# A hybrid SSD and S5 decoder step on one core: modulation blocks moved into the scan, the last group norms moved between output projection groups

## The chip, the core and the metric

The kernel runs on one core of a Trainium2 chip. A core has five engines that work side by side, each through its own queue in order: TensorE (PE, matmuls; its weight loads are shown apart as PEld), VectorE (DVE), ScalarE (ACT), GpSimd (POOL) and SyncE (SP, which here issues all DMAs). The metric is the device time of one execution in microseconds (us); lower is better.

## The reference, cut to what matters

One layer of a decoder for 1024 prompt tokens (one sequence) and 8 x 4 sample tokens, D = 1024, together 1056 columns. Everything is float32.

```python
mod = (silu(c) @ w_ada + b_ada)              # 6 x 1024 per sequence: sh1, sc1, g1, sh2, sc2, g2
u = rmsnorm(x, norm1_g) * (1 + sc1) + sh1
proj = u @ w_in                              # z, xBC, dt and the S5 input
y_ssd = ssd_mixer(...)                       # conv, scan over 8 chunks of 128 tokens, * silu(z)
y_ssd = y_ssd * rsqrt(mean(y_ssd^2) + eps) * norm_g     # group norm: 2 groups of 256 channels
y_s5 = s5_mixer(...)                         # complex diagonal scan, gelu, then the glu below
y_s5 = g * sigmoid(g @ w_glu + b_glu)
x = x + g1 * (concat(y_ssd, y_s5) @ w_out)   # output projection, 1024 x 1024
v = rmsnorm(x, norm2_g) * (1 + sc2) + sh2
x = x + g2 * ((silu(v @ w_gate) * (v @ w_up)) @ w_down)  # FFN, width 2816
y = rmsnorm(x, normf_g) * (1 + scf) + shf    # modulated by a second, smaller projection of c
```

## The kernel before

Every large product of float32 matrices is done as three matmuls: both factors are split into a high and a low part (high by an ACT copy, low by a subtraction on POOL or DVE), and high x high, high x low and low x high are summed in PSUM. The 1056 columns are worked in four blocks b of NB = 264 columns.

The stages and where they lie in the profiled execution: input norm and projection (up to about 240 us), S5 (to about 325 us), the last part of the SSD scan with its group norms and the glu of the S5 half (to 472.8 us), output projection (472.8 to 589.6 us), first FFN tile by a fast matrix product (7 products instead of 8; Strassen type, `ORD`), and then ten more FFN tiles `gu(j, mat)`, the down projection and the last norm.

What the change touches:

- The modulation. `mod` has 64 columns of 128 rows here (48 of the layer, 16 of the last norm). A block is loaded by `ada_load` (512 KB; name `arw` in the scan, one buffer; `ar` in the output projection, two buffers), multiplied by `ada_mm` (8 matmuls, then an ACT copy to `adasb`) and finished by `ada_fin` (one small matmul with a selection matrix, and one DVE instruction that adds c1 and multiplies by gs). In the scan `ada_a` does the first half of the block loaded last and issues the next load, `ada_b` does the second half. In the output projection `ada_dc` does the same in the middle of a group, at its matmul 12.
- The scan. `ssd_r`, `ssd_a` and `ssd_b` are the three parts of chunk c; `ssd_b(7)` is the last. `gn_sq(b)` squares and sums the gated scan output (`gac`), `gn_stat(b)` sums over channels with 6 matmuls and takes 1/sqrt on DVE by Newton steps (`rq_m`, `rq_i`, `rq_t`, result `grs`), `gn_out(b, g)` spreads `grs` over the partitions with matmuls and scales (`gf`, then the split `m` for the output projection). `glus` does n glu units (12 matmuls, a tanh on ACT named `sg`, DVE and POOL).
- The output projection. `out_group(w, m, b)` is 24 matmuls for 128 output rows and 264 columns, then `residual` (`x<-mm,mod,x` on DVE, which needs the tile `x` reloaded by `x<-xT`) and a square for the next norm. `w_out` comes in four pieces i of 1 MB.
- The first FFN tile and its successor. `dn_sums(j)` loads a piece of `w_down` and forms sums of its quarters on DVE (`ts`), which are written to memory. `gu_forms` loads 1 MB of gate or up weights (`raw<-w_gu`, `raw` has two buffers), forms sums on DVE (`arw` again) and splits them into slots that are taken in the order of the list `WS` (names `wl`, `wh`, `wf`, `wg`).

From the scan on, PE's order is that of the code (`tc.manual_schedule` for PE alone); the orders of DVE, ACT, POOL and SP are set by a scheduler, which works from a simulated time line. Pools are opened and closed in code order, and a tile whose place is reused waits for the last use of the old one.

## Time and profile before

Three runs: median 1320.55 us, 1320.35 to 1320.65. The profiled execution took 1317.78 us: a span of 1316.0 us and 1.78 us around it.

| | busy us | share of the span |
|---|---|---|
| PE | 1232.2 | 94% |
| PEld | 1165.4 | 89% |
| DVE | 891.2 | 68% |
| POOL | 630.8 | 48% |
| ACT | 505.3 | 38% |

The mean granted TensorE clock is 0.971 of full speed. PE is the engine to watch: it is idle for 83.8 us, and it is slowed where the clock is below 1.00. Idle time of another engine means nothing by itself; what matters is which of them PE waited for in a stretch. In the timeline a bracket gives the idle time before the instruction and what ended it.

### The profile page before, as it was taken

What the parts mean: (1) busy time and instruction counts of PE and PEld (TensorE: products, weight loads), DVE (VectorE), ACT (ScalarE), POOL (GpSimd) and SP (SyncE); (2) the same over time, 40 slices, a digit from 0 to 9 for tenths busy, and PEclk for the clock granted to TensorE, in tenths of its full rate; (3) what the DMA queues carried; (4) which work ended last, traced back from release to release, by engine and by line L of the source; (5) the groups of instructions that cost most, each with busy time, mean ns of one, the idle gap of its engine ahead of it and who ended that gap; (6) DMA issues with size and microseconds to landing.
All of it is one profiled execution on the core that took longest, in us unless ns stands there. A gap on an engine that the chain in (4) does not pass through costs nothing.

```text
span 1316.0 us, 26191 instructions
## 1 busy us (share of the span) xinstructions
PE 1232.2 (94%) x10165; PEld 1165.4 (89%) x10165; DVE 891.2 (68%) x1757; ACT 505.3 (38%) x1000; POOL 630.8 (48%) x626
## 2 busy tenths in 40 slices
...
GB/s 339 177 99 158 108 97 130 147 160 241 116 161 81 107 137 214 202 108 6 158 165 178 154 132 193 154 178 154 135 127 186 124 234 200 200 184 188 212 104 133
DMA packets 203741, 206.57 MB, mean 157 GB/s; under 512 B 12128, under 2 KB 177504, under 8 KB 199264
## 3 DMA queue, kind: packets, MB, share of 16 engines
...
## 4 chain that ended last, share of the span: by engine, by line
PE 64%; DVE 19%; DMA 6%; POOL 5%; issue 3%; ACT 2%; SPq 1%; ACTq 0%; DVEq 0%; POOLq 0%
PE mm L1508 45%; PE mm L120 13%; PE ps L120 3%; POOL tr L105 2%; DVE tp L105 2%; POOL W L105 1%; DVE xo L114 1%; PE nb L120 1%; DVE m L105 1%; DVE R L105 1%; DVE gf L105 1%; DVE E L105 1%; POOL wl L105 1%; PE pa L120 1%; DMA ts<-hd 1%
## 5 line engine op out<-in xcount | busy, mean ns | idle before, releaser
L1508 PE MATMUL mm<-m,wh 128*128 128x264 f32 x1376 | 190.1, 285 | 1.6 <-DVE ue L105 1.6
L1508 PEld LDWEIGHTS mm<-m,wh 128*128 128x128 f32 x1376 | 176.6, 188 | 2.2 <-DVE ue L105 1.8
L1508 PE MATMUL mm<-m,wg 128*128 128x264 f32 x802 | 113.7, 289 | 7.9 <-ACT wg L117 7.9
L1508 PEld LDWEIGHTS mm<-m,wg 128*128 128x128 f32 x802 | 105.5, 192 | 8.4 <-ACT wg L117 8.3
L105 POOL TENSOR_TENSOR wl<-raw,wh 128x1024 fp32r<-128x1024 f32 x24 | 59.8, 2491 | 91.3 <-ACT wh L117 51.8
L1508 PE MATMUL mm<-m,wf 128*128 128x264 f32 x670 | 90.8, 284 | 0.0
L1508 PEld LDWEIGHTS mm<-m,wf 128*128 128x128 f32 x670 | 85.2, 188 | 0.2 <-DVE g L105 0.2
L105 POOL TENSOR_TENSOR wl<-arw,wl 128x512 fp32r<-128x512 f32 x40 | 56.1, 1403 | 57.3 <-ACT wl L117 57.3
L1508 PE MATMUL mm<-v,wl 128*128 128x264 f32 x586 | 83.4, 285 | 0.0
L120 PE MATMUL mm<-uh,wh 128*128 128x384 f32 (+1 forms) x360 | 77.5, 341 | 4.9 <-ACT uh L117 4.4
L1508 PE MATMUL mm<-w,wl 128*128 128x264 f32 x570 | 81.3, 284 | 0.0
L120 PE MATMUL mm<-m,wh 128*128 128x264 f32 x512 | 77.2, 299 | 1.6 <-ACT sg L117 1.3
L1508 PEld LDWEIGHTS mm<-v,wl 128*128 128x128 f32 x586 | 76.5, 188 | 0.0
L120 PE MATMUL mm<-uh,wl 128*128 128x384 f32 (+1 forms) x360 | 74.5, 332 | 0.0
L1508 PEld LDWEIGHTS mm<-w,wl 128*128 128x128 f32 x570 | 74.3, 188 | 0.0
L120 PEld LDWEIGHTS mm<-m,wh 128*128 128x128 f32 x512 | 69.4, 199 | 4.6 <-issue 2.8
L120 PE MATMUL mm<-ul,wh 128*128 128x384 f32 (+1 forms) x360 | 71.8, 327 | 1.3 <-POOL ul L105 1.2
L117 ACT ACTIVATE wh<-raw 128x1024 fp32r<-128x1024 f32 (+2 forms) x60 | 50.2, 837 | 58.2 <-PE mm L1508 26.8
L120 PEld LDWEIGHTS mm<-uh,wh 128*128 128x128 f32 x360 | 60.8, 193 | 13.2 <-issue 6.9
L105 POOL TENSOR_TENSOR wg<-raw,wg 128x512 fp32r<-128x512 f32 (+2 forms) x32 | 49.6, 1549 | 37.1 <-ACT wg L117 23.5
L105 DVE TENSOR_TENSOR m<-ts,m 128x528 fp32r<-128x528 f32 (+1 forms) x50 | 42.0, 858 | 33.0 <-ACT m L117 32.6
L120 PEld LDWEIGHTS mm<-ul,wh 128*128 128x128 f32 x360 | 59.4, 189 | 4.0 <-POOL ul L105 2.8
...
## 6 DMA issues: line engine op xcount, KB each, us to landing
...
ts<-hd SPq DMA_DIRECT2D x70, 264.0 KB, 3.7
arw<-w_ada SPq DMA_DIRECT2D x27, 512.0 KB, 4.3
...
ar<-w_ada SPq DMA_DIRECT2D x21, 512.0 KB, 4.5
...
```

What stands on the lines that cost most here:

```text
L105: e.tensor_tensor(o, a, b, op)
L114: V.scalar_tensor_tensor(o, a, s, b, o0, o1)
L117: S.activation(o, a, f, bias=bias, scale=scale)
L120: T.matmul(o, l, r, start=start, stop=stop)
L1508: T.matmul(o, wv[k][1 if s == 2 else 0], xv[k][1 if s == 1 else 0], start=first and s == 0 and k == 0, stop=(s == 2 and k == n - 1), skip_ ...
```

## The change

- Modulation: seven more `ada_a`/`ada_b` pairs stand in the scan, two more `ada_a` (on another PSUM bank) between the first output groups; 35 blocks go through `arw` instead of 27, 13 through `ar` instead of 21. `ada_dc` stands in fewer output groups. The last step of a single block is an ACT instruction (scale gs, bias cg = c1 * gs) instead of a DVE one.
- The end of the scan: early scan tiles get a pool of their own, `sde`, closed after `ssd_a(7)`; in its place the first piece of `w_out` is loaded and split during the scan (low part on DVE: `v<-raw,v`). `gn_stat(2)` and all after it go into the output projection's block, with four output groups (i = 0, b = 0 and 1) between them, and `gn_out` inside these groups. Statistics are taken in pieces of 88 columns, so that no piece needs padding.
- FFN start: `dn_sums(0)` comes after `gu(1, 0)`, and `WS` begins with the slots `wl`, `wh`, `wl`, `wf` where it began with `wg`, `wg`.
- At the end `ahead(n, mp)` is called in the loop instead of ahead of it. The orders of SP and DVE there are the same as before.

The diff, cut (the left out parts give tiles of the early scan to `sde`, and take the square sums in blocks of NB columns):

```diff
--- before.py
+++ after.py
...
@@ -186,7 +187,8 @@
         d = mod[:, m0:m0 + n, :]
         sh = [128, n, 9]
         if n == 1:
-            ts(d, o, c1[:, m0:m0 + 1], P["gs"][:, m0:m0 + 1], add, mult)
+            o, d = o[:, 0], d[:, 0]
+            act(d, o, AF.Identity, bias=cg[:, m0:m0 + 1], scale=P["gs"][:, m0:m0 + 1])
...
-    def ada_a():
+    def ada_a(own=True):
 
         m = ada_next[0]
         if ada_raw[0] is not None:
-            ada_open[0] = (m, 1) + ada_mm(ada_raw[0], 1)
+            ada_open[0] = (m, 1) + ada_mm(ada_raw[0], 1, "pa" if own else psm())
             m = ada_next[0] = m + 1
         ada_raw[0] = ada_load(m, 1, st, "arw", 1)[0] if m < 64 else None
 
...
+    sde = pool("sde", side="right")
...
         if c == 8:
-            return tl(sd, shape, tag + "8")
+            return tl(sde, shape, tag + "8")
...
@@ -1102,7 +1106,10 @@
             else:
                 tt(V, hn.rearrange("p (h q) -> p h q", q=64), hprev.rearrange("p (h q) -> p h q", q=64),
                    eAt[:, 8 * c:8 * c + 8].unsqueeze(2).to_broadcast([128, 8, 64]), mult)
-                tt(V, hn, hn, pst, add)
+                if c == 7:
+
+                    hn = tl(gl, [128, 8, 136], "gq").rearrange("p i n -> p (i n)")[:, 0:512]
+                tt(V, hn, hprev, pst, add)
...
-        sg = tl(gl, [128, 384], "sg", bufs=2)[:, 0:w]
+        sg = tl(gl, [128, NB], "sg", bufs=2)
         act(sg, o[:, 0:w], AF.Tanh, bias=bg2[:, m:m + 1], scale=0.5)
         act(sg, sg, AF.Copy, 0.5, 0.5)
-        gf = tl(gl, [128, 384], "gf", bufs=2)[:, 0:w]
+        gf = tl(gl, [128, NB], "gf", bufs=3)
...
     def gn_stat(b):
...
-        rs = tl(gl, [128, 6], "grs", bufs=2)
-        rsqrt(rs, p1[:, 384:396].rearrange("p (c z) -> p c z", z=2)[:, :, 0], 6, 1.0 / 256)
+                mm(p1[0:88, 384 + i:385 + i], GN[b][g][:, 88 * c:88 * c + 88], ones[:, 0:1])
+        rs = tl(gl, [128, 6], "grs", bufs=2)[0:88, :]
+        for _ in rsqrt_steps(rs, p1[0:88, 384:396].rearrange("p (c z) -> p c z", z=2)[:, :, 0], 6, 1.0 / 256, rows=88):
+            pass
         GN[b] = rs
 
-    def gn_out(b, g):
-        c0, w = NB * b, NB
+    def gn_out(b, g, pt="nb"):
         rs = GN[b]
-        pb = nbt()
+        pb = nbt(pt)
         for c in range(3):
-            n = min(128, w - 128 * c)
-            mm(pb[:, 128 * c:128 * c + n], rs[:, 3 * g + c:3 * g + c + 1].to_broadcast([128, 128]), ident[:, 0:n])
+            mm(pb[:, 88 * c:88 * c + 88], rs[:, 3 * g + c:3 * g + c + 1].to_broadcast([88, 128]), ident[0:88, 0:88])
         for i in range(2):
             m = 2 * g + i
-            gf = tl(gl, [128, 384], "gf", bufs=2)[:, 0:w]
-            stt(gf, yT[:, m, c0:c0 + w], P["norm_g"][:, m:m + 1], pb[:, 0:w], mult, mult)
+            gf = tl(gl, [128, NB], "gf", bufs=3)
+            stt(gf, yT[:, m, NB * b:NB * b + NB], P["norm_g"][:, m:m + 1], pb[:, 0:NB], mult, mult)
             act(mx(0, m, b), gf, AF.Copy)
             tt(G, mx(1, m, b), gf, mx(0, m, b).bitcast(F32), sub)
 
...
+    def x2_load(i):
+        for hh in range(2):
+            for n in range(2):
+                dma(x2[n][:, 2 * i + hh, :], A["xT"][2 * i + hh][:, 528 * n:528 * n + 528])
+
+    def out_weights(i):
+
+        raw = raw_tile()
+        dma(raw, A["w_out"][i])
+        if i:
+            x2_load(i)
+        return [split_h(raw, h, V if i < 2 else G, None if i in (1, 2) else [tl(vb0, [128, 4 * NB], f"v{2 * h + q}", F32R)[:, 0:1024]
+                                                            for q in range(2)]) for h in range(2)]
 
...
         glu_in(0)
         ssd_yd(8)
         h = ssd_b(1, h)
+        ada_a()
         ssd_a(2)
+        ada_b()
         ssd_r(3, PV)
         glu_in(1)
         ada_a()
+        ssd_a(3)
         ada_b()
-        ssd_a(3)
         ssd_r(4, PV)
         smp_turn(0)
         glu_in(2)
         ada_a()
         h = ssd_b(2, h)
+        ada_b()
         gn_sq(0)
         smp_state(0, (0, 1))
+        ada_a()
         smp_state(0, (2, 3))
         smp_load(1)
         glu_in(3)
         ada_b()
         ssd_a(4)
+        ada_a()
         ssd_r(5, PV)
         gn_stat(0)
         h = ssd_b(3, h)
+        ada_b()
         ssd_r(6, PV)
         ada_a()
         ssd_a(5)
@@ -1316,12 +1347,16 @@
         glus(wg, 1)
         ada_b()
         smp_out(1)
+        ada_a()
         h = ssd_b(4, h)
         smp_turn(1)
+        ada_b()
         glus(wg, 1)
         ada_a()
         ssd_a(6)
+        ada_b()
         smp_state(1, (2, 3))
+        ada_a()
         ssd_r(7, PV)
         smp_state(1, (0, 1))
         ada_b()
@@ -1335,6 +1370,9 @@
         glus(wg, 2)
         ada_a()
         ssd_a(7)
+        close("sde")
+        vb0 = pool("vb0")
+        wo0 = out_weights(0)
         gn_stat(1)
         ada_b()
         h = ssd_b(6, h)
@@ -1344,31 +1382,14 @@
         ada_b()
         h = ssd_b(7, h)
         gn_sq(3)
-        gn_stat(2)
-        gn_out(1, 1)
-        gn_out(1, 0)
-        glus(wg, 2)
-        gn_stat(3)
-        gn_out(2, 0)
-        gn_out(2, 1)
-        glus(wg, 2)
-        gn_out(3, 0)
-        gn_out(3, 1)
+        ada_a()
     dma(O["ssdp"], h)
-    ada_next[0] += 1
-    ada_fin(ada_next[0] - 1, 1, *ada_mm(ada_raw[0], 1))
-    ada_more(40 - ada_next[0])
     close("sd")
...
+        ws = {0: wo0}
+        x2_load(0)
+        gn_stat(2)
+        ada_b()
+        out_group(ws[0][0], 0, 0, {8: lambda: gn_out(1, 0, "pa"), 18: lambda: gn_out(1, 1)})
+        ada_a(False)
+        out_group(ws[0][1], 1, 0, {4: lambda: gn_out(2, 0, "pa"), 14: lambda: gn_out(2, 1)})
+        gn_stat(3)
+        ada_b()
+        glus(wg, 2)
+        out_group(ws[0][0], 0, 1)
+        ada_a(False)
+        glus(wg, 2)
+        ada_b()
+        out_group(ws[0][1], 1, 1, {4: lambda: gn_out(3, 0, "pa"), 14: lambda: gn_out(3, 1)})
+
         AQ, AO = [], []
+        ada_next[0] += 1
+        AO.append((ada_next[0] - 1, 1) + ada_mm(ada_raw[0], 1))
+        close("gl")
+        close("yp")
+        hpA = pool("hpA", side="right")
+        arp = pool("ar", side="right")
 
...
-        ws = {}
+        for _ in range(2):
+            ada_get()
         for i in range(4):
-            if i < 3:
-                ws[i] = pair(A["w_out"][i])
-            else:
-                raw = raw_tile()
-                dma(raw, A["w_out"][i])
-                ws[i] = [split_h(raw, h, G, [tl(vb0, [128, 4 * NB], f"v{2 * h + q}", F32R)[:, 0:1024] for q in range(2)])
-                         for h in range(2)]
-            for hh in range(2):
-                for n in range(2):
-                    dma(x2[n][:, 2 * i + hh, :], A["xT"][2 * i + hh][:, 528 * n:528 * n + 528])
-            if i == 0:
-                for _ in range(2):
-                    ada_get()
-            for b in range(4 if i < 2 else 2):
+            if i:
+                ws[i] = out_weights(i)
+            for b in ((2, 3), (0, 1, 2, 3), (0, 1), (0, 1))[i]:
                 for hh in range(2):
-                    out_group(ws[i][hh], 2 * i + hh, b, {12: ada_dc} if i else None)
+                    out_group(ws[i][hh], 2 * i + hh, b, {12: ada_dc} if i and 64 - ada_next[0] > (0, 13, 9, 5)[i] else None)
         root_table(x2[0][:, 0, 0:1])
...
-        WS += [(hpB, "wg", 2), (hpB, "wg", 2), (st, "wl", 2), (st, "wh", 2), (st, "wl", 2), (hpA, "wf", 1), (st, "wh", 2)]
-        dn_sums(0)
+        WS += [(st, "wl", 2), (st, "wh", 2), (st, "wl", 2), (hpA, "wf", 1), (hpB, "wg", 2), (hpB, "wg", 2), (st, "wh", 2)]
 
...
                 gu(j, mat, gu_forms(j, mat), PRE if j + mat == NP else {})
                 if mat and j < NP - 1:
                     dn_sums(j)
-                if (j, mat) == (5, 0):
-                    dn_sums(NP - 1)
+                if mat == 0 and j in (1, 5):
+                    dn_sums(0 if j == 1 else NP - 1)
 
...
-            if last:
-                for n in range(2):
-                    for mp in range(4):
-                        ahead(n, mp)
...
+                if last:
+                    ahead(n, mp)
...
```

PE after the last scan chunk, before (`ps` the chunk's own products, `nb` the group norm, `pa` a modulation block, `mm<-m` a glu unit):

```order
L120 MATMUL ps_4898<-E_4690,Xdt_4722 64x128 x4
L120 MATMUL ps_4898<-E_4695,Xdt_4722 64x128 x4
L120 MATMUL nb_4928<-ones_79,gac_4779 128x1 x3
L120 MATMUL nb_4928<-ones_79,gac_4785 128x1 x3
L120 MATMUL pa_5132<-arw_4802,cs_82 32x128 x8
L120 MATMUL nb_4951<-cst_75,grs_4735 128x128 x2
L120 MATMUL nb_4951<-cst_75,grs_4735 128x8
L120 MATMUL pa_5132<-cst_75,adasb_5141 128x9
L120 MATMUL nb_4963<-cst_75,grs_4735 128x128 x2
L120 MATMUL nb_4963<-cst_75,grs_4735 128x8
L120 MATMUL mm_4975<-m_486_3819,wh_3852 128x264
L120 MATMUL mm_4975<-m_488_3821,wh_3852 128x264
```

And with the change, from the same statistics on (`v_730` is the high part of the first piece of `w_out`):

```order
L120 MATMUL nb_5072<-ones_79,gac_4869 88x1 x3
L120 MATMUL nb_5072<-ones_79,gac_4874 88x1 x3
L120 MATMUL pa_5015<-cst_75,adasb_5024 128x9
L120 MATMUL mm_5097<-m_486_3823,v_730_4810 128x264
L120 MATMUL mm_5097<-m_488_3825,v_730_4810 128x264
L120 MATMUL mm_5097<-m_490_3827,v_730_4810 128x264
L120 MATMUL mm_5097<-m_492_3829,v_730_4810 128x264
L120 MATMUL mm_5097<-m_494_3831,v_730_4810 128x264
L120 MATMUL mm_5097<-m_496_3833,v_730_4810 128x264
L120 MATMUL mm_5097<-m_498_3835,v_730_4810 128x264
L120 MATMUL mm_5097<-m_500_3837,v_730_4810 128x264
L120 MATMUL nb_5106<-cst_75,grs_4825 128x88 x3
```

The statistics of block 2 now stand behind a modulation block instead of ahead of it, and an output group with a `gn_out` inside follows, where two `gn_out` and a glu unit followed.

DVE at the end of the statistics of block 2 (`rq_t`, `rq_i`, `grs`), before:

```order
L105 TENSOR_TENSOR gac_4916<-gac_4916,sq_4919 128x264
L114 SCALAR_TENSOR_TENSOR gf_4967<-yT_3423,par_77,nb_4963 128x264
L114 SCALAR_TENSOR_TENSOR rq_i_4938<-rq_t_4937,rq_i_4938 128x6
L114 SCALAR_TENSOR_TENSOR gf_4971<-yT_3423,par_77,nb_4963 128x264
L105 TENSOR_TENSOR gac_4922<-gac_4922,sq_4925 128x264
L114 SCALAR_TENSOR_TENSOR rq_t_4937<-rq_i_4938 128x6
L105 TENSOR_TENSOR rq_t_4937<-rq_t_4937,rq_m_4936 128x6
L114 SCALAR_TENSOR_TENSOR grs_4935<-rq_t_4937,rq_i_4938 128x6
```

And with the change:

```order
L105 TENSOR_TENSOR gac_5005<-gac_5005,sq_5007 128x264
L114 SCALAR_TENSOR_TENSOR gf_5132<-yT_3425,par_77,nb_5128 128x264
L114 SCALAR_TENSOR_TENSOR rq_t_5081<-rq_i_5082 88x6
L114 SCALAR_TENSOR_TENSOR gf_5136<-yT_3425,par_77,nb_5128 128x264
L105 TENSOR_TENSOR gac_5010<-gac_5010,sq_5012 128x264
L114 SCALAR_TENSOR_TENSOR x_772_5041<-mm_5097,mod_84,x_772_5041 128x264
L105 TENSOR_TENSOR rq_t_5081<-rq_t_5081,rq_m_5080 88x6
L114 SCALAR_TENSOR_TENSOR grs_5079<-rq_t_5081,rq_i_5082 88x6
L114 SCALAR_TENSOR_TENSOR gf_5170<-yT_3425,par_77,nb_5166 128x264
```

The residual of the first output group, `x_772<-mm`, stands ahead of the last two steps to `grs`.

SP where the first FFN tile ends, before:

```order
L93 DMA raw_7216<-w_dn 128x16x128
L93 DMA hd_5174<-g_977_6627 128x264
L93 DMA hd_5176<-gx_979_6660 128x264
L93 DMA hd_5178<-g_983_6714 128x264
L93 DMA hd_5175<-g_1019_6855 128x264
L93 DMA hd_5177<-gx_1021_6886 128x264
L93 DMA raw_7230<-w_gu 128x2048
L93 DMA hd_5179<-g_1025_6940 128x264
```

And with the change:

```order
L93 DMA raw_7215<-w_gu 128x2048
L93 DMA hd_5048<-g_979_6626 128x264
L93 DMA hd_5050<-gx_981_6659 128x264
L93 DMA hd_5052<-g_985_6713 128x264
L93 DMA hd_5049<-g_1021_6854 128x264
L93 DMA hd_5051<-gx_1023_6885 128x264
L93 DMA raw_7447<-w_dn 128x16x128
L93 DMA hd_5053<-g_1027_6939 128x264
```

The load of the next gate weights and that of the down weights have changed places.

## Rows read from the trace of the kernel before

**Rows 1.** Windows: from:to, length, busy PE, PEld, DVE, ACT, POOL; PEclk, DMA share, GB/s.

```profile
325.00:415.00 90.00, 74.51 (x690) 59.85 (x690) 77.89 (x130) 37.90 (x73) 64.55 (x54) 0.90 0.44 134
415.00:470.00 55.00, 48.48 (x390) 45.60 (x390) 45.25 (x115) 24.94 (x62) 26.32 (x28) 0.82 0.25 83
520.00:530.00 10.00, 8.03 (x77) 7.55 (x76) 3.56 (x6) 2.57 (x6) 2.37 (x1) 0.83 0.44 121
610.00:660.00 50.00, 41.59 (x311) 41.14 (x310) 38.34 (x42) 15.08 (x30) 27.96 (x18) 0.90 0.38 118
660.00:860.00 200.00, 200.00 (x1638) 199.81 (x1638) 141.56 (x225) 63.32 (x128) 103.80 (x78) 1.00 0.51 159
```

**Rows 2.** Waits of PE from 320 to 480 us: total, times, longest.

```profile
PE nb L120 <- DVE rq_m L111: 4.3, 2, 2.4
...
PE nb L120 <- DVE gf L114: 2.1, 2, 1.4
...
PE pa L120 <- DMA arw<-w_ada: 0.3, 1, 0.3
```

**Rows 3.** Timeline of PE, 442 to 482 us: start, length, line, operation, count, [idle before].

```profile
449.74 1.42 PE L120 MATMUL nb<-cst,grs 128*128 128x128 f32 x6 [1.90 <-DVE rq_m L111]
...
462.74 1.45 PE L120 MATMUL nb<-cst,grs 128*128 128x128 f32 x6 [2.45 <-DVE rq_m L111]
465.62 1.42 PE L120 MATMUL nb<-cst,grs 128*128 128x128 f32 x6 [1.43 <-DVE gf L114]
...
472.81 2.21 PE L120 MATMUL mm<-m,wh 128*128 128x264 f32 x16 [1.26 <-ACT sg L117]
```

**Rows 4.** Timeline of PE, 488 to 530 us, in the output projection.

```profile
490.81 2.11 PE L120 MATMUL mm<-m,wh 128*128 128x264 f32 x16
...
493.74 2.13 PE L120 MATMUL mm<-m,wh 128*128 128x264 f32 x16
...
509.41 0.29 PE L120 MATMUL mm<-cst,adasb 128*128 128x9 f32 x2
...
510.20 0.76 PE L120 MATMUL mm<-m,wh 128*128 128x264 f32 x4
...
522.98 0.64 PE L120 MATMUL mm<-ar,cs 128*32 128x128 f32 x16 [1.97 <-DMA ar<-w_ada]
```

**Rows 5.** Timeline of SP's queue, 430 to 500 us.

```profile
452.01 4.54 SPq L93 DMA_DIRECT2D x<-xT  x8
```

**Rows 6.** DMA issues from 430 to 480 us: count, size, median us to landing.

```profile
x<-xT SPq DMA_DIRECT2D x8, 264.0 KB, 4.6
```

**Rows 7.** Timeline of DVE, 440 to 485 us.

```profile
457.31 0.17 DVE L114 SCALAR_TENSOR_TENSOR grs<-rq_t,rq_i 128x6 f32<-128x6 f32 x1
```

**Rows 8.** Timeline of PE, 605 to 664 us, first FFN tile to the next.

```profile
648.68 5.30 PE L1508 MATMUL mm<-m,wg 128*128 128x264 f32 x24 [5.53 <-ACT wg L117]
656.86 3.01 PE L1508 MATMUL mm<-v,wg 128*128 128x264 f32 x12 [2.89 <-ACT wg L117]
```

**Rows 9.** Timeline of SP's queue, 615 to 660 us.

```profile
624.14 0.38 SPq L93 DMA_DIRECT2D raw<-w_dn  x1
...
642.70 0.33 SPq L93 DMA_DIRECT2D raw<-w_gu  x1
```

**Rows 10.** Timeline of ACT, 640 to 664 us.

```profile
648.00 0.63 ACT L117 ACTIVATE wg<-raw 128x512 fp32r<-128x512 f32 x1 [4.35 <-DMA raw<-w_gu]
```

**Rows 11.** Groups of DVE instructions by line and form: count, busy us, mean ns.

```profile
L111 DVE TENSOR_SCALAR mod<-pa,c,par 128x9 f32<-128x9 f32 x27 | 7.6, 281 | 30.0 <-PE pa L120 24.9 <-ACT Vq L117 5.1
...
L105 DVE TENSOR_TENSOR wl<-raw,wh 128x1024 fp32r<-128x1024 f32 x3 | 3.7, 1226 | 0.0
```

**Rows 12.** The page's DMA issues, the whole execution.

```profile
arw<-w_ada SPq DMA_DIRECT2D x27, 512.0 KB, 4.3
```

**Rows 13.** Timeline of ACT, 584 to 605 us.

```profile
593.61 1.28 ACT L117 ACT_TABLE_LOAD   x1
594.90 0.39 ACT L117 ACTIVATE g<-mm 128x264 f32<-128x264 f32 x1
```

More of the change, by code (lines that the diff above doesn't have):

```diff
@@ L133, in build @@
     c1 = tl(cp, [128, 64], "c1")
+    cg = tl(cp, [128, 64], "cg")
     cs = tl(cp, [128, 8, 32], "cs")
@@ L551, in build @@
                 og[0, 0] = e0
+    tt(V, cg, c1, P["gs"], mult)
     og = [og[hh, b] for hh in range(2) for b in range(3)]
@@ L1005, in ssd_r @@
             for p, d in enumerate((dAh.bitcast(F32), dAl) if c < 8 else (dA,)):
-                R = tl(sd, [128, 4, 128], "R", F32R if c < 8 else F32, bufs=4)[0:n, :, 0:n]
+                R = tl(sde, [128, 4, 128], "R", F32R if c < 8 else F32, bufs=4)[0:n, :, 0:n]
                 tt(eng[2 * g + p], R, ml.unsqueeze(1).to_broadcast([n, 4, n]),
@@ L1063, in ssd_a @@
         if c == 8:
-            s["Bm"] = [tl(sd, [128, 2, 128], "Bm"), Bt]
+            s["Bm"] = [tl(sde, [128, 2, 128], "Bm"), Bt]
             for q in range(2):
@@ L1126, in smp_load @@
         for b in range(4 * q, 4 * q + 4):
-            HS[b] = tl(sd, [128, 512], "hs", bufs=4)
+            HS[b] = tl(sde, [128, 512], "hs", bufs=4)
             dma(HS[b], A["h0T"][b])
@@ L1137, in smp_out @@
                    HS[4 * q + j][:, 256 * g:256 * g + 256])
-        pos = s["po"] = tl(sd, [128, 512], "pos")
+        pos = s["po"] = tl(sde, [128, 512], "pos")
         act(pos, po, AF.Copy)
@@ L1223, in gn_sq @@
     def gn_sq(b):
-        c0, w = NB * b, NB
         GN[b] = []
         for g in range(2):
-            acc = tl(gl, [128, 384], "gac", bufs=2)
+            acc = tl(gl, [128, NB], "gac", bufs=2)
             for i in range(2):
-                sq_acc(acc, yT[:, 2 * g + i, c0:c0 + w], w, i == 0, V)
+                src = yT[:, 2 * g + i, NB * b:NB * b + NB]
+                if i:
+                    sq = tl(cp, [128, 384], "sq", bufs=2)[:, 0:NB]
+                    act(sq, src, AF.Square)
+                    tt(V, acc, acc, sq, add)
+                else:
+                    act(acc, src, AF.Square)
             GN[b].append(acc)
```

8 lines of the change are left out of this document (1 added, 7 removed).

## The prediction

> **What bounds the kernel now.** I read the windows by stage first, then PE's waits in the two stretches that the change touches, and last the timelines of PE, DVE, SP and ACT there. The windows show where PE can gain at all [rows 1]: from 660 to 860 us it is busy for all of 200 us at the full clock, so whatever is saved or lost ahead of 660 reaches the end unchanged. In the scan PE is idle for 15.5 of 90 us (325 to 415) while DVE is busy for 77.9, and for 6.5 of 55 us (415 to 470) at a mean clock of 0.82; between 610 and 660 it is idle for 8.4 of 50 us at 0.90. These stretches are limited by latency: PE waits for DVE's 1/sqrt steps and the scaling behind them (4.3 and 2.1 us) [rows 2], and then works on at the lower of its two clock levels, 1.2 GHz. A modulation block's load is hardly waited for there, 0.3 us [rows 2].
>
> **FFN start.** The tile after the first FFN tile waits 5.53 and 2.89 us for a split weight, and its 24 matmuls take 5.30 us, the next 12 take 3.01 [rows 8]. A group of 24 at the full clock takes 2.93 us, from 490.81 to 493.74 [rows 4]; so the slow clock costs 2.37 and 3.01 - 1.47 = 1.54 us more, and the place loses 5.53 + 2.89 + 2.37 + 1.54 = 12.3 us. The reason is in SP's queue: at 624.14 the free `raw` buffer goes to the down weights, and the load that PE needs is issued at 642.70 [rows 9] and releases ACT's first split at 648.00 [rows 10]. The change exchanges the two loads and moves the down sums on DVE behind the tile. The load of 5.3 us (642.70 to 648.00) then starts near 624 and is there near 630, 13 us before PE runs dry; its sums meet a DVE that is idle for 11.7 of 50 us [rows 1]. The first three slots are those of the tile's first weights, already used up; the fourth, `wf`, is in use until the tile ends, but PE then has three products of 2.93 us ahead of it against one ACT split of 0.63 [rows 10] and a subtraction. What is late next is a second sum or a slot; I leave 0.8 us for it: **-11.5 us**, between -12.3 (nothing left) and -2 (another slot or sum takes over).
>
> **End of the scan.** The idle time ahead of 449.74 begins at 447.84, where the modulation block has ended. Before, PE does the rest of the group norms and four glus until 472.81, and then begins the output groups [rows 3]; four of these and the last `gn_out` put the same work at 472.81 + 4 x 2.93 + 0.7 = 485.2. A `gn_out` takes 1.42 us at the slow clock, so 0.7 at the full one [rows 3]; a glu is half a group, 1.47; a statistic I take like a `gn_out` at the slow clock, 1.4, since its matmuls are one column wide. The work is 6 x 0.7 + 4 x 1.47 + 1.4 + 0.2 + 4 x 2.93 = 23.4 us in 37.4, so 14 are lost, 7.75 of them idle: 1.90, 2.45, 1.43 and 1.26 [rows 3], and 0.7 more for `gf` [rows 2]. With the change the same work, the statistic of block 2 and two modulation blocks (0.79 each, from 509.41 to 510.20 [rows 4]) follow in one line: 23.4 + 1.4 + 1.6 = 26.4 us, at the full clock 474.2. An output group now covers most of each 1/sqrt chain.
>
> It doesn't cover all. DVE has the first group's residual ahead of the last steps to `grs`, and this residual needs `x`, whose loads are issued from 452.01 [rows 5], when the last scan chunk is gated, and land after a median of 4.6 us [rows 6]: 456.6, and 0.8 for the residual and two steps makes 457.4; before, `grs` came at 457.31 [rows 7]. PE needs it at 447.84 + 1.4 + 0.2 + 2.93 + 1.4 + 0.6 + 0.5 = 454.9, so it waits some 2.5 us. Behind a wait of 1.97 us the clock fell to a mean of 0.83 over ten microseconds, 1.7 us of time [rows 4, 1]; so I take 5 us for the wait and what the clock costs behind it, and 1.3 for one more wait for a glu's tanh, as at 472.81. That gives 480.5: **-4.7 us**, between -11 (no new wait) and 0 (the chains take as long as now). Behind the residual all of DVE's work for the next `gn_out` is queued, and PE waits for that.
>
> **Fewer blocks later.** Seven blocks go into the scan and two between the first groups, so the later groups lose nine: 9 x 0.79 = **-7.1 us** on a PE that is otherwise full. The wait of 1.97 us at 522.98 for such a load costs 3.7 with the clock; with blocks in fewer groups I take half: **-1.9**, between -3.7 and 0.
>
> **In the scan** the seven blocks cost PE 7 x 0.79 = 5.5 us beside 22 us of idle time [rows 1], but some stand ahead of products that DVE waits for: **+2**, between 0 and +7 (all exposed, with waits for the loads). DVE loses the last step of the blocks, 0.281 us each, eight in that stretch before, and gains two splits of 1.226 us [rows 11]: -2.2 + 2.5, nothing. The new ACT steps lie on an engine that is busy for 37.9 of 90 us [rows 1]; were DVE's relief to reach PE, it would be -2, and +1 if the new steps delay a tanh. The pool, the 88-column pieces and the end's `ahead` add no work in these rows; they are at 0 with the same two ends.
>
> **Tables.** The square root that loads ACT's table for the second norm now lies between tanhs, so there are two more table loads, one ahead of the first of the last glus and one ahead of the second norm's square root. A load takes 1.28 us, and the next instruction starts 0.01 us behind it [rows 13]: **+0.6**, between 0 (hidden behind matmuls) and 2 x 1.28. The Trainium skill (ScalarE: Activation LUTs, What ACT_TABLE_LOAD costs) counts about 2.66 us for a switch, with a drain of some 1.38 behind the load; by it this term would have its upper end at 5.3 and the forecast, in the same proportion, would be 0.6 us later. No such drain stands between the two rows here.
>
> **Sum.** -11.5 - 4.7 - 7.1 - 1.9 + 2 + 0.6 = -22.6 us on the profiled execution of 1317.78 (span 1316.0 and 1.78 around it): 1295.2. That execution lies 2.77 below the median of the runs, 1320.55, so on the median's scale the forecast is **1298 us**.
>
> **The rivals.**
> - *The group norms' waits are replaced by new ones.* The residual's wait for `x` and the long DVE queue take all that the new order gives, and the blocks cost 4 us in the scan: -11.5 - 7.1 + 4 + 0.6 = -14, 1306.5 us. For it: DVE is the busy engine of the scan, and `grs` comes no sooner than now. Against it: three of the four waits have an output group in front of them now.
> - *Everything is hidden.* -12.3 - 11 - 7.1 - 3.7 and nothing added: -34, 1286.5. For it: an idle PE of 22 us in the scan. Against it: the residual's place in DVE's queue.
> - *The FFN start doesn't gain,* because a sum on DVE or a slot of the first tile is as late as the load was: -2 in place of -11.5, 1307.5. Against it: DVE's idle time there.
> - *The loads stall PE, and the kernel is slower.* `arw` has one buffer, and a load of 512 KB takes 4.3 us to land [rows 12]; a block that comes before it is there holds PE, the clock falls, and DVE's chain in the scan waits for PE. At 3.7 us each, as at 522.98, nine added blocks would cost 33 us and outweigh the -24.6 that the other terms give without the scan's: 9 us slower in all, 1329. It decides from seven such stalls on. For it: SP issues in order, so a load behind another that still waits for its buffer comes late. Against it: before, the blocks of that stretch waited 0.3 us in all [rows 2], and 15 blocks in 145 us leave 9.7 us for a load.
>
> **Chances.** Forecast 0.52, new waits 0.18, all hidden 0.12, no gain at the FFN 0.06, stalled loads 0.12, of which 0.03 near the balance point and 0.09 beyond. A change below 0.2% (2.6 us) can't be told from none here. That makes faster 0.88, same 0.03, slower 0.09. The likeliest case alone spans 1291 to 1304; the range takes in the rivals on the fast side and reaches 1314, where the worst ends of the scan and of the norms come together (-8 at the FFN, 0 at the norms, -7.1, +7, +2, about -6). So 1285 to 1314.
>
> **What would show it.** PE's waits for a split weight after the first FFN tile gone, and the tile's first 24 matmuls in about 2.9 us; if they aren't, the FFN term is wrong. In the output projection's first groups one wait of 2 to 3 us for `grs` of block 2 with a slower clock behind it, and the fourth group ended near 480 us plus what the scan gained or lost; no wait there means the all-hidden rival, several mean the first. The second half of the output projection free of a wait for `ar`. PE's wait for `arw` in the scan below 3 us in all; if it is 10 or more, the last rival holds. The forecast is wrong if the scan up to its last chunk is later by more than 7 us, or if the first tile's end moves less than 5 us ahead of now.

## The result, and the profile after

The changed kernel takes 1307.57 us (median of 4 runs, 1299.44 to 1312.46) against 1320.45: ratio 0.988, 95% interval 0.984 to 0.992. It is faster, by 13 us between the medians and 16 by the ratio, where 22.5 was forecast, and its runs differ by 13 us where those of the kernel before beside them differed by one. That one is a small sample: in the sessions of the experiments the kernel before spread over 5 to 10 us in 11 or 17 runs. The profiled execution took 1304.18 us, span 1302.4.

To see where the time went, both traces are cut at the same PE instructions. A cut is the start of the matmul group that the row names (first or last of its name; the first FFN tile is cut at its last `mm<-m,raw`; the last row runs to the end of the last matmul), so each difference belongs to one stage. The columns to the right are the experiments below; `again` and `again2` are the changed kernel unedited.

| us, from cut to cut | before | after | again | again2 | blocks_back | s5_dve | mod_dve | norms_only | ffn_only | sums_late | both_late | best | both_late_mod |
|---|---|---|---|---|---|---|---|---|---|---|---|---|---|
| start to last `ps<-CP` | 202.5 | 206.6 | 203.3 | 201.7 | 200.6 | 204.9 | 205.7 | 200.9 | 203.3 | 202.5 | 203.6 | 208.3 | 207.1 |
| to last `ps<-H,CP` (S5) | 70.3 | 72.0 | 79.1 | 72.0 | 71.9 | 69.3 | 70.3 | 79.5 | 70.3 | 71.5 | 70.6 | 69.8 | 69.6 |
| to first scan chunk | 58.8 | 59.4 | 61.6 | 58.9 | 59.3 | 58.6 | 58.4 | 61.5 | 61.5 | 59.5 | 59.5 | 58.4 | 58.7 |
| to last scan chunk | 111.2 | 111.6 | 112.7 | 111.6 | 111.7 | 114.3 | 115.9 | 112.4 | 112.4 | 112.8 | 110.5 | 114.6 | 116.7 |
| to first FFN tile | 146.8 | 130.5 | 130.6 | 130.4 | 135.4 | 130.8 | 129.5 | 130.7 | 147.4 | 130.3 | 130.7 | 131.0 | 129.6 |
| that tile | 52.4 | 52.4 | 52.5 | 52.4 | 52.4 | 52.4 | 52.4 | 52.4 | 52.4 | 52.4 | 52.4 | 52.4 | 52.4 |
| to PE's wait for `ue` | 423.1 | 418.7 | 417.2 | 417.1 | 420.2 | 421.1 | 420.6 | 422.5 | 420.5 | 416.9 | 410.7 | 410.9 | 411.0 |
| to the last matmul | 243.2 | 243.5 | 243.8 | 242.4 | 243.9 | 244.5 | 243.9 | 245.2 | 245.3 | 244.7 | 244.2 | 243.9 | 244.1 |

Read down the second column: 16.4 us are won between the scan and the FFN, 4.4 at the FFN start, 0.5 are lost in the scan, and 6.4 are lost ahead of it, where the prediction had no term. Each column is one execution: stages that two kernels have in common differ by some 2 us among them in the scan, 4 in the FFN and 8 at the start.

The windows at the same times, to be held against [rows 1]; a stage lies 6 to 7 us later in the scan here, and about 10 us earlier from the first FFN tile on (from:to, length, busy PE, PEld, DVE, ACT, POOL; PEclk, DMA share, GB/s):

```profile
325.00:415.00 90.00, 77.94 (x781) 63.06 (x780) 73.55 (x115) 45.48 (x92) 66.20 (x55) 0.94 0.59 177
415.00:470.00 55.00, 49.98 (x431) 44.99 (x432) 46.87 (x104) 26.61 (x68) 26.32 (x27) 0.88 0.41 131
610.00:660.00 50.00, 47.32 (x375) 46.79 (x374) 38.66 (x46) 16.63 (x33) 29.42 (x19) 0.97 0.48 151
660.00:860.00 200.00, 196.52 (x1605) 195.95 (x1604) 147.00 (x231) 62.11 (x126) 105.52 (x79) 1.00 0.53 166
```

PE is no longer full behind 660 us: 196.52 of 200, where [rows 1] had 200. Its timeline from 630 to 700 us, which answers to [rows 8], shows why (start, length, line, operation, count, [idle before]):

```profile
633.45 3.08 PE L1529 MATMUL mm<-m,wl 128*128 128x264 f32 x24
...
655.76 1.82 PE L1529 MATMUL mm<-m,wh 128*128 128x264 f32 x12 [2.63 <-DVE g L105]
...
674.53 3.41 PE L1529 MATMUL mm<-m,wg 128*128 128x264 f32 x24 [0.89 <-DVE g L105]
...
696.62 1.72 PE L1529 MATMUL mm<-w,wg 128*128 128x264 f32 x12 [2.59 <-DVE gu L105]
```

The waits of 5.53 and 2.89 us for `wg` are gone, and the first 24 matmuls of the tile stand at 633.45, right behind the tile before. In their place are three waits for a PSUM bank that DVE has yet to empty (`g`, `gu`). What DVE and SP did ahead of the first of them:

```profile
652.84 0.69 DVE L105 TENSOR_TENSOR arw<-raw 128x512 f32<-128x512 f32 x1 [4.66 <-DMA raw<-w_gu]
653.45 0.42 DVE L105 TENSOR_TENSOR gx<-gx,mm 128x264 f32<-128x264 f32 x1
653.79 1.58 DVE L105 TENSOR_TENSOR arw<-arw,raw 128x512 f32<-128x512 f32 x1
655.29 0.42 DVE L105 TENSOR_TENSOR g<-gx,mm 128x264 f32<-128x264 f32 x1
```

```profile
643.82 2.63 SPq L93 DMA_DIRECT2D wd<-ts  x4
646.54 0.56 SPq L93 DMA_DIRECT2D raw<-w_gu  x1
647.15 0.67 SPq L93 DMA_DIRECT2D raw<-w_dn  x1
```

DVE stood still for 4.66 us on `arw<-raw`, a sum that needs the weights of gu(1, 1); the instructions that empty PSUM banks, `gx<-gx,mm` and `g<-gx,mm`, stand behind it in the queue, and PE's wait ends with the second. SP issued that load at 646.54. Two things held it back. The `raw` buffer that came free first, at the end of the first FFN tile, went to the down weights, and the other one was read by POOL for gu(1, 0) until 642.89:

```profile
633.15 0.38 SPq L93 DMA_DIRECT2D raw<-w_dn  x1
641.40 1.49 POOL L105 TENSOR_TENSOR wg<-raw,wg 128x512 fp32r<-128x512 f32 x1
```

From 642.89 on, the writes of dn_sums(0), `wd<-ts`, which wait for DVE's `ts`, stand ahead of the load in SP's queue. So the buffer cost the load 9.7 us (633.15 to 642.89) and the writes at most 3.7 more; no run has the one without the other. The stall has moved by one load, from a load that the down sums delay to the next load, which they delay as well.

Around the group norms, against [rows 2] and [rows 3], PE's waits from 449 to 582 us, the whole of them:

```profile
PE nb L120 <- DVE gac L105: 1.6, 2, 0.9
PE nb L120 <- DVE grs L114: 0.9, 1, 0.9
PE mm L120 <- DVE Ec L105: 0.4, 1, 0.4
```

They were 9.7 us in that stage before. The wait for `grs` of block 2 is there, but 0.9 us long. The residual ahead of it on DVE (464.68) didn't wait for `x`, which SP issued from 459.48:

```profile
464.68 0.48 DVE L114 SCALAR_TENSOR_TENSOR x<-mm,mod,x 128x264 f32<-128x264 f32 x1
465.08 0.31 DVE L105 TENSOR_TENSOR rq_t<-rq_t,rq_m 88x6 f32<-88x6 f32 x1
465.43 0.74 DVE L114 SCALAR_TENSOR_TENSOR grs<-rq_t,rq_i 88x6 f32<-88x6 f32 x1
```

The granted clock was low ahead of that wait, behind the waits for `gac`, and back at 1.00 behind it; the fourth output group ended at 485.73, with the matmuls of the last line:

```profile
455.00:460.00 5.00, 4.15 (x22) 4.06 (x23) 4.77 (x14) 0.78 (x2) 2.01 (x2) 0.59 0.47 149
460.00:465.00 5.00, 5.00 (x43) 4.66 (x43) 3.78 (x12) 2.68 (x9) 2.03 (x3) 0.73 0.83 268
465.00:470.00 5.00, 4.05 (x34) 3.87 (x34) 2.84 (x8) 3.34 (x9) 2.56 (x4) 1.00 0.76 247
```

```profile
484.27 1.46 PE L120 MATMUL mm<-m,v 128*128 128x264 f32 x10
```

### The profile page after: what moved, and what is told of

Its sections match the earlier page's. It is cut to its first block, busy times and chain, and to the rows that moved or that the text cites. A ratio compares the mean times of both kernels' runs of the same rounds, so it can differ in the third digit from the quotient of the medians.

```text
span 1302.4 us, 26177 instructions
## 1 busy us (share of the span) xinstructions
PE 1229.6 (94%) x10165; PEld 1162.1 (89%) x10165; DVE 884.4 (68%) x1706; ACT 521.9 (40%) x1050; POOL 619.3 (48%) x622
## 4 chain that ended last, share of the span: by engine, by line
PE 64%; DVE 20%; POOL 5%; DMA 5%; issue 3%; ACT 2%; SPq 0%; ACTq 0%; DVEq 0%; POOLq 0%
PE mm L1529 44%; PE mm L120 13%; PE ps L120 4%; POOL tr L105 2%; DVE tp L105 2%; DVE xo L114 2%; POOL W L105 1%; DMA xad<-xo 1%; PE pa L120 1%; PE nb L120 1%; DMA raw<-w_gu 1%; DVE gf L105 1%; DVE Ec L114 1%; DVE E L105 1%; DVE g L105 1%
## 5 line engine op out<-in xcount | busy, mean ns | idle before, releaser
L1529 PE MATMUL mm<-m,wl 128*128 128x264 f32 x890 | 127.8, 288 | 2.9 <-DVE m L1487 1.7
L1529 PE MATMUL mm<-m,wh 128*128 128x264 f32 x894 | 126.1, 285 | 4.2 <-DVE g L105 2.6
L1529 PEld LDWEIGHTS mm<-m,wl 128*128 128x128 f32 x890 | 117.2, 191 | 3.6 <-DVE m L1487 1.9
L1529 PEld LDWEIGHTS mm<-m,wh 128*128 128x128 f32 x894 | 115.7, 188 | 4.9 <-DVE g L105 2.8
L1529 PE MATMUL mm<-m,wg 128*128 128x264 f32 x771 | 106.0, 285 | 0.9 <-DVE g L105 0.9
L105 POOL TENSOR_TENSOR wh<-arw,wh 128x512 fp32r<-128x512 f32 x40 | 54.8, 1369 | 42.6 <-ACT wh L117 42.6
L114 DVE SCALAR_TENSOR_TENSOR xo<-rw,par,xo 128x1024 f32<-128x1024 f32 (+1 forms) x48 | 38.2, 841 | 35.2 <-ACT xo L117 35.2
L105 DVE TENSOR_TENSOR arw<-raw 128x512 f32<-128x512 f32 x40 | 42.3, 1057 | 27.9 <-POOL wh L105 13.9
L120 PEld LDWEIGHTS mm<-uh,wl 128*128 128x128 f32 x360 | 59.8, 190 | 1.1 <-issue 0.8
L105 POOL TENSOR_TENSOR wl<-raw,wl 128x512 fp32r<-128x512 f32 (+1 forms) x30 | 42.1, 1402 | 37.9 <-ACT wl L117 37.9
L120 PE MATMUL mm<-m,wh 128*128 128x264 f32 x384 | 54.6, 290 | 0.0
```

The source lines that it names most:

```text
L105: e.tensor_tensor(o, a, b, op)
L114: V.scalar_tensor_tensor(o, a, s, b, o0, o1)
L120: T.matmul(o, l, r, start=start, stop=stop)
L1529: T.matmul(o, wv[k][1 if s == 2 else 0], xv[k][1 if s == 1 else 0], start=first and s == 0 and k == 0, stop=(s == 2 and k == n - 1), skip_ ...
```

## The experiments

**again** and **again2**: the changed kernel, nothing edited, in two sessions.

> The changed kernel once more, nothing edited. Its four times lie from 1299.4 to 1312.5 us while those of the kernel before lie within 1 us, so something in it isn't fixed. Theory A: the spread arises in the first 330 us, where the profiled run was already 6.4 us later than the kernel before at the first scan chunk; then this profile's span differs from 1302.4 by about what its first scan chunk (ps<-Xd,Bt) differs from 338.0 us, and the rest from there to the end (964.4 us) is the same within 2 us. Theory B: it arises in the new waits of the output projection and the FFN; then the first chunk is again near 338 and the rest differs by 3 us or more. Median between 1300 and 1312 by both.

> The changed kernel unedited beside the two above, on the same chip. By theory A its times spread over 8 us or more again, with some runs below 1302 and more above 1306; by the rival it spreads as s5_dve does.

Medians 1308.70 (1299.69 to 1313.01, 6 runs; ratio 0.988, 0.985 to 0.991) and 1304.52 (1295.93 to 1312.40, 6 runs; ratio 0.988, 0.984 to 0.992). The profiled run of `again` is 6.0 us later than the first one at the first scan chunk (344.0 against 338.0), and its span is 6.0 us longer, 1308.4: theory A holds for the place. The runs of `again2` spread over 16.5 us, two below 1302 and three above 1306, as its theory A said. Most of the 6.0 us lies in the S5 stage, 79.1 against 72.0 us. PE's timeline in `again` there, and the windows:

```profile
223.16 0.70 PE L120 MATMUL ps<-H,CP 64*128 64x136 f32 x6 [1.45 <-DVE H L105]
```

```profile
220.00:230.00 10.00, 8.55 (x46) 6.17 (x44) 9.86 (x20) 1.96 (x4) 2.49 (x4) 0.71 0.19 54
230.00:240.00 10.00, 10.00 (x32) 8.38 (x32) 0.16 (x1) 4.16 (x7) 0.23 (x2) 0.50 0.13 54
```

and the same windows in the changed kernel's first profile, where PE's wait at that place was 1.61 us (in the kernel before, 0.59):

```profile
220.00:230.00 10.00, 8.38 (x65) 6.91 (x63) 9.86 (x18) 3.72 (x7) 3.42 (x3) 1.00 0.34 113
230.00:240.00 10.00, 10.00 (x58) 8.43 (x58) 3.58 (x12) 3.97 (x7) 0.25 (x2) 1.00 0.28 97
```

Behind the wait the granted clock is 0.71 and then 0.50 in `again`, that is, the engine fell to 1.2 GHz, and 1.00 throughout in the other run of the same kernel. The stage was some 7 us longer with the fall than without.

The wait goes with DVE's order there, though not always (see both_late). In the kernel before, these lines lead to `H`:

```profile
212.31 0.68 DVE L105 TENSOR_TENSOR g<-tp,tp 128x512 f32<-128x512 f32 x1
213.02 1.29 DVE L105 TENSOR_TENSOR tp<-W,Vq 128x512 f32<-128x512 f32 x2
...
217.50 3.48 DVE L105 TENSOR_TENSOR tp<-W,g 128x512 f32<-128x512 f32 x2
221.01 0.70 DVE L105 TENSOR_TENSOR H<-tp,tp 128x512 f32<-128x512 f32 x1
```

In the changed kernel a pair of convolution steps, `xo`, stands between them:

```profile
215.85 0.68 DVE L105 TENSOR_TENSOR g<-tp,tp 128x512 f32<-128x512 f32 x1
216.45 1.43 DVE L114 SCALAR_TENSOR_TENSOR xo<-rw,par,xo 128x1024 f32<-128x1024 f32 x2
217.81 1.28 DVE L105 TENSOR_TENSOR tp<-W,Vq 128x512 f32<-128x512 f32 x2
...
222.27 3.46 DVE L105 TENSOR_TENSOR tp<-W,g 128x512 f32<-128x512 f32 x2
225.77 0.70 DVE L105 TENSOR_TENSOR H<-tp,tp 128x512 f32<-128x512 f32 x1
```

**ffn_only** is the kernel before with the last part alone.

```diff
-        WS += [(hpB, "wg", 2), (hpB, "wg", 2), (st, "wl", 2), (st, "wh", 2), ...]
-        dn_sums(0)
+        WS += [(st, "wl", 2), (st, "wh", 2), (st, "wl", 2), (hpA, "wf", 1), ...]
...
-                if (j, mat) == (5, 0):
-                    dn_sums(NP - 1)
+                if mat == 0 and j in (1, 5):
+                    dn_sums(0 if j == 1 else NP - 1)
```

> The kernel before with the FFN start of the change alone: the new order of the slots, and dn_sums(0) behind gu(1, 0). Theory A (read from the profile after): the wait for the weights of gu(1, 0) goes, but the writes of dn_sums(0) stand in SP's queue ahead of the load of gu(1, 1), DVE waits for that load with PSUM evacuations queued behind it, and PE waits 2 to 3 us each at two or three places up to 700 us; about -4.4 us, 1316. Rival (the prediction's step): the place is simply free, -11.5 us, 1309, and the profile shows no PE wait over 1 us from 640 to 860 us.

1318.47 (1314.77 to 1322.56, 12 runs; 1323.02 beside it; ratio 0.9965, 0.9949 to 0.9981): -4.6 us. The stretch behind the first FFN tile took 420.5 us, -2.6. Theory A on the waits, and on the size within the scatter; the prediction's -11.5 falls. The waits are those of the changed kernel, without anything else of it:

```profile
670.53 1.94 PE L1508 MATMUL mm<-m,wh 128*128 128x264 f32 x12 [2.72 <-DVE g L105]
...
689.18 3.42 PE L1508 MATMUL mm<-m,wg 128*128 128x264 f32 x24 [0.82 <-DVE g L105]
...
707.88 1.72 PE L1508 MATMUL mm<-v,wg 128*128 128x264 f32 x12 [0.65 <-DVE gu L105]
711.85 2.27 PE L1508 MATMUL mm<-w,wg 128*128 128x264 f32 x12 [2.25 <-DVE gu L105]
```

**norms_only** is the reverse, the changed kernel with the old FFN start.

> The changed kernel with the FFN start as before: modulation blocks, pools, the group norms between output groups. Theory A: from the scan's last chunk to the first FFN tile it gains the 16.4 us that the profile after shows, the scan costs 0.5, and the 6.4 us lost in the first 330 us come and go from run to run; 1304 to 1312 with a spread of several us. Rival: the early loss belongs to the change (one more DVE instruction and another schedule there), is there in every run, and the median is near 1310 with a spread below 2 us. The first tile after the first FFN tile waits 5 and 3 us for wg by both.

1312.39 (1302.67 to 1314.33; ratio 0.990, 0.987 to 0.993). From the scan to the FFN 130.7 us, behind it 422.5 with the old waits of 5.61 and 2.96 us for `wg`. Theory A on the stages and on the spread of 12 us, with a median at the upper end of its range; this run too had the long S5 stage (79.5). Against the kernel before in the same session the two halves of the change make -10.6 and -4.6 us, together -15.2, and the whole change in `again` made -14.3.

**sums_late** moves dn_sums(0) further back.

```diff
-                if mat == 0 and j in (1, 5):
-                    dn_sums(0 if j == 1 else NP - 1)
+                if mat == 0 and j in (5, 8):
+                    dn_sums(0 if j == 8 else NP - 1)
```

> The changed kernel with dn_sums(0) behind gu(8, 0) instead of gu(1, 0). Theory A: the writes and loads of dn_sums(0) are what makes the load of gu(1, 1) late; without them PE has no wait for DVE g or gu from 640 to 710 us, and the kernel is 6 to 8 us faster than the changed one (2.63 + 0.89 + 2.59 us of waits and about 2 us of slow clock). Rival: DVE's own load in that tile, or the two raw buffers, set those waits whoever uses them; then they stay within 1 us of 6.1 in sum and the time is that of the changed kernel.

1299.66 (1298.52 to 1303.39; ratio 0.982, 0.980 to 0.985). Neither theory in full. The three waits became one, of 4.35 us, and the stretch took 416.9 us, only 0.1 to 1.8 less than in the three profiles of the changed kernel; so this stretch doesn't explain a median 9 us below that of `again` beside it. Runs without the long S5 stage would explain most of it, and fit the spread of 5 us, but only one of the six has a profile. With dn_sums(0) out of the way, the load of gu(1, 1) was issued as soon as the first FFN tile ended (629.71); the next free `raw` buffer got the weights of dn_sums(1) (640.20), whose four `ts` DVE then did ahead of the bank:

```profile
647.89 0.68 DVE L105 TENSOR_TENSOR ts<-raw 128x512 f32<-128x512 f32 x1
648.61 0.69 DVE L105 TENSOR_TENSOR ts<-ts,raw 128x512 f32<-128x512 f32 x1
649.22 1.75 DVE L105 TENSOR_TENSOR ts<-raw 128x512 f32<-128x512 f32 x1
650.89 0.41 DVE L105 TENSOR_TENSOR gx<-gx,mm 128x264 f32<-128x264 f32 x1
651.23 0.68 DVE L105 TENSOR_TENSOR ts<-raw,ts 128x512 f32<-128x512 f32 x1
651.83 0.42 DVE L105 TENSOR_TENSOR g<-gx,mm 128x264 f32<-128x264 f32 x1
```

```profile
652.30 5.65 PE L1529 MATMUL mm<-m,wh 128*128 128x264 f32 x24 [4.35 <-DVE g L105]
```

**both_late** moves dn_sums(1) too.

```diff
-                if mat and j < NP - 1:
+                if mat and 1 < j < NP - 1:
                     dn_sums(j)
-                if mat == 0 and j in (1, 5):
-                    dn_sums(0 if j == 1 else NP - 1)
+                if mat == 0 and j in (5, 7, 8):
+                    dn_sums({5: NP - 1, 7: 1, 8: 0}[j])
```

> The changed kernel with dn_sums(0) behind gu(8, 0) and dn_sums(1) behind gu(7, 0). In sums_late PE still waited once, 4.35 us, for DVE's g, with the sums of dn_sums(1) ahead of it in DVE's queue. Theory A: any down sums near that tile do this; without both, no PE wait from 640 to 710 us, and the stretch from the end of the first FFN tile to the wait for ue near 1046 takes 411 us (416.9 in sums_late, 418.7 in the changed kernel, 423.1 before): the whole 12 us. Rival: DVE is late there by its own work (the combinations ta, tb, tc after the first tile take 1.2 us each), so a wait of 2 us or more stays and the stretch takes 415 or more.

1294.42 (1291.59 to 1303.97; ratio 0.981, 0.978 to 0.983). The stretch took 410.7 us, 12.4 less than before, as large as the whole loss that the prediction had read from [rows 8], and 410.9 and 411.0 in the two other kernels with both sums late. Theory A, but for one wait of 0.87 us that is left:

```profile
646.91 3.17 PE L1529 MATMUL mm<-m,wh 128*128 128x264 f32 x24 [0.87 <-DVE g L105]
```

The load of gu(1, 1) takes the buffer that goes to the down weights at 633.15 in the changed kernel, as soon as the first FFN tile ends:

```profile
627.90 0.33 SPq L93 DMA_DIRECT2D raw<-w_gu  x1
```

In the S5 stage DVE's order is that of the changed kernel, with `xo` ahead of `H`, and yet PE has no wait over 0.2 us for `H`: here the two `tp<-W,g` ahead of `H` take 1.26 us and not 3.46. The six runs still spread over 12.4 us.

```profile
218.56 1.26 DVE L105 TENSOR_TENSOR tp<-W,g 128x512 f32<-128x512 f32 x2
219.86 0.69 DVE L105 TENSOR_TENSOR H<-tp,tp 128x512 f32<-128x512 f32 x1
```

**blocks_back** takes five of the added modulation blocks out of the scan (five `ada_a`/`ada_b` pairs, at `ssd_b(1)`, `gn_sq(0)`, `ssd_a(4)`, `smp_out(1)` and `ssd_a(6)`); `ada_dc` picks them up in the output groups.

> The changed kernel with five of the added modulation blocks taken out of the scan again; they go back into the output groups. Theory A: from the last scan chunk to the first FFN tile it takes 130.5 + 5 x 0.79 = 134.5 us (146.8 before), and the scan from first to last chunk is up to 1 us shorter than 112; so the rest of the gain there, 12 us, is the group norms' order alone. Rival: the blocks fill PE's waits in the scan and keep its clock up, so without them the scan takes 114 us or more. Second rival: the loads of ar come to be waited for again, 2 to 4 us more, 137 or more.

1308.71 (1304.68 to 1311.90; ratio 0.989, 0.987 to 0.991). The output stage took 135.4 us, 5.0 more for five blocks, between theory A and its second rival (0.6 us of it is a wait for `ar`). The scan was as long, 111.7 against 111.6: within its scatter, these five blocks cost nothing there.

**mod_dve** puts the last step of a block back on DVE, everywhere; **both_late_mod** does so in both_late.

```diff
-            o, d = o[:, 0], d[:, 0]
-            act(d, o, AF.Identity, bias=cg[:, m0:m0 + 1], scale=P["gs"][:, m0:m0 + 1])
+            ts(d, o, c1[:, m0:m0 + 1], P["gs"][:, m0:m0 + 1], add, mult)
...
```

> The changed kernel with the last step of a modulation block back on DVE (no cg). Theory A: with that step on ACT the scheduler puts a 1.44 us DVE instruction (the convolution's xo) later in the S5 stage, so PE waits 1.45 to 1.62 us for H at 222 us instead of 0.59, and in some runs the clock falls to half behind it for some 15 us, 8 us lost; undone, the wait is 0.6 again, no run has the slow stretch, and the median falls from 1308 to about 1301 with a spread below 6 us. In the scan DVE gets its steps back: 0 to 2 us slower there. Rival: the slow stretch comes from the loads at the start, whatever the order on DVE; then median and spread are those of the changed kernel, 1308 and 13 us.

> Both edits together: the step of a modulation block on DVE, and both down sums late. If the two causes are independent, the time is the changed kernel's less 8 us of slow stretch where that comes and 7 to 8 us at the FFN: 1292 to 1296, spread below 6 us. Rival: with DVE busier in the scan the group norms' chain gets longer and takes back 3 us or more, 1297 to 1300.

1306.58 (1303.94 to 1307.20, 4 runs; ratio 0.987, 0.985 to 0.989) and 1297.28 (1295.64 to 1298.47, 4 runs; ratio 0.981, 0.979 to 0.982). PE's wait for H at that place is 0.42 us in the one and absent in the other, the S5 stage takes 70.3 and 69.6 us, and the spread is 3 us: theory A there. But the scan takes 115.9 and 116.7 us, 4 to 5 more, so the medians are not those of the theories: 1306.58 and not 1301, and 1297.28, the rival's time. In mod_dve, PE's waits from 325 to 480 us begin with

```profile
PE pa L120 <- DVE mod L111: 9.6, 6, 4.2
```

where the changed kernel had 0.7 us for `mod` on ACT. A block's PSUM bank `pa` is single, so the next block's matmuls wait until DVE, busy for 97.4 of the 115.9 us, comes to the last step.

**s5_dve** keeps that step on DVE up to the scan and on ACT from there; **best** adds both late sums.

```diff
-        if n == 1:
+        if n == 1 and not in_scan[0]:
+            ts(d, o, c1[:, m0:m0 + 1], P["gs"][:, m0:m0 + 1], add, mult)
+        elif n == 1:
...
```

> The changed kernel with the modulation step on DVE up to the scan, and on ACT from there on. DVE's order in the S5 stage is then that of the kernel before. Theory A: the wait for H at 222 us is 0.6 us again and no run has the slow stretch of some 8 us behind it, so the times lie between 1298 and 1305 us; the scan keeps its 112 us from first to last chunk (116 with all of these steps on DVE). Rival: the slow stretch belongs to the loads at the start; then times up to 1312 come as often as with the changed kernel.

> The same with dn_sums(1) and dn_sums(0) behind gu(7, 0) and gu(8, 0). If the three causes add up: wait for H 0.6 us, scan 112, last scan chunk to first FFN tile 130.5, end of the first FFN tile to the wait for ue 411 us; 1290 to 1295 with a spread below 6 us, 3 us below both_late's median or as fast as its fastest run, 1291.6.

1304.08 (1300.44 to 1306.25, 5 runs; ratio 0.987, 0.985 to 0.990) and 1298.77 (1294.85 to 1300.31, 5 runs; ratio 0.982, 0.980 to 0.985). None of the 18 runs of the four kernels with the step on DVE in S5 (these two, mod_dve and both_late_mod) lies more than 2.2 us above its kernel's median; of the changed kernel's 16 runs some lie 4 to 8 us above theirs in each session, and on the chip of these two kernels `again2` went up to 1312.40. S5 took 69.3 and 69.8 us. That fits theory A. It doesn't make the wait the source of the scatter: the kernel before, whose wait is short, spread over 9.4 us in 17 runs of one session, both_late without the wait over 12.4, and sums_late with a wait of 1.62 us over 4.9. Nor did the median gain: s5_dve's 1304.08 stands beside 1304.52 of `again2`. The scan took 114.3 and 114.6 us instead of the 112 expected, so `best` missed its 1290 to 1295 and is no better than both_late (ratios 0.982 and 0.981, intervals overlapping). Since the step is on ACT in the scan here, only some 2 of the 4 to 5 us that mod_dve and both_late_mod lose in the scan belong to the step on DVE; why it is some 3 us longer in s5_dve and `best` as well was not tried.

## Why the prediction was right or wrong

The direction was right, and 1298 lies 10 us under the measured median, inside the range of 1285 to 1314. Errors of both signs are in that. In the profile, against the -22.6 of the sum, the FFN start came out 7.1 us worse and 6.4 us were lost ahead of the scan, where no term stood; the end of the scan with the output stage came out 2.7 better, the scan 1.5 better, and the tables' 0.6 didn't show (with 0.3 at the end, -13.6 in all). By steps:

- *FFN start, -11.5: wrong, and this is the step that failed.* It held that the load would come early (it did: the wait for `wg` is gone) and that "What is late next is a second sum or a slot; I leave 0.8 us for it". Next was a second sum, as it said, but it cost far more than 0.8: the sum waited for the second load, of gu(1, 1), which came late because the down weights had the buffer and the writes of their sums stood ahead of it in SP's queue; DVE's queue carried the delay to PSUM and PE. The gain was 2.0 to 6.0 us in the seven profiles with this FFN start (4.4 in the first), so 6 to 10 of 12.4 us were taken back. ffn_only shows it alone, both_late shows the full gain once the sums are gone from there. The argument that DVE was idle for 11.7 of 50 us was about DVE's load and not about what stood ahead in its queue.
- *End of the scan and output stage, -4.7 - 7.1 - 1.9 = -13.7: right, a little small;* measured -16.4. The fourth output group ended 36.1 us behind the last scan chunk, where the prediction had 42.4 for the old order (485.2 - 442.8) and 37.7 for the new: -6.3 for its -4.7. The rest made -10.0 for its -9.0. blocks_back gives the blocks' share: 5.0 us for five, 1.0 each with a wait for `ar` and 0.88 without, against 0.79; the wait for `ar` of the kernel before went entirely. The mechanism of the first term was right in part. The wait for `grs` was sized at 2.5 us and was 0.95, and no slow clock followed it; the slow clock came ahead of it, behind 1.6 us of waits for `gac` that the prediction didn't have. `x` was there in time, and PE waited for no tanh.
- *In the scan, +2: a little large,* -0.7 to 1.6 in the six profiles that keep this part and DVE's order in S5, and 3.1 and 3.4 in s5_dve and best. ffn_only, with the old scan, has 1.2, so these sizes are near the scatter. That blocks hide in PE's waits is shown for five of them by blocks_back. That the step taken off DVE is worth nothing was wrong for another reason than DVE's load: on DVE it holds the single bank `pa`, and PE waits 9.6 us for it in mod_dve, some 2 us of which reach the end of the scan (115.9 against 114.3 in s5_dve). The loads of `arw` were waited for 3.7 us in all, between the forecast's bound of 3 and the 10 of the last rival.
- *Tables, +0.6: nothing to see.* PE waited for no tanh; the load at 471.93 took 1.28 us and the next ACT instruction began 0.01 us later, so here too nothing stood between the two.
- *Ahead of the scan: no term.* The prediction followed the step that moves from DVE to ACT in the scan only. In S5 the scheduler gave DVE another order, with a pair of convolution steps of 1.43 us ahead of `H`, and PE's wait went from 0.59 us to between 1.45 and 1.62 in six of the seven profiles with that step on ACT; in two of the six the clock fell behind it, some 7 us. That the order makes the wait longer is supported by mod_dve (0.42 us with the old order); both_late shows that it doesn't always. That the wait makes the clock fall rests on two profiles of thirteen. The other part of the profiled run's 6.4 us, 4.1 ahead of the S5 stage, is the start's own scatter: 200.6 to 208.3 over the profiles, with no order by kernel.

By the sign that the prediction itself set, a last scan chunk later by more than 7 us, it was 6.8 us later in the first profile (449.65 against 442.82) and 13.8 in `again` (456.63); but the time was lost ahead of the scan and not in it.

The rival nearest to what happened is the third, that the FFN start doesn't gain because a sum on DVE is as late as the load was. The gain lies between its -2 and the forecast's -11.5, and the cause is a sum on DVE; it had a chance of 0.06, and DVE's idle time, which was held against it, didn't help. That its 1307.5 us meets the measured 1307.57 is luck: it has neither the loss ahead of the scan nor the larger gain at the norms. New waits at the norms came too, but took less than the old ones; the stalled loads did not come.
